# Sixteen instead of twelve places for the norms' small tiles: every later operand lies 128 bytes further on

## The chip, the cores and the metric

The kernel runs on one core of one Trainium2 chip. The metric is the device time of one execution in microseconds, as the median of several runs. TensorE is called PE (its weight loads PEld), VectorE DVE, ScalarE ACT, GpSimd POOL and SyncE SP.

## The reference, cut to what matters

Two layers over 512 tokens of width 1024. Each layer is a half SwiGLU block, a mixer (RWKV-7 with memory attention in the first layer, dilated attention with memory attention in the second), and a second half SwiGLU block:

```python
def swiglu_ffn(x, norm_g, w_in, w_out):
    gate, up = jnp.split(rms_norm(x, norm_g) @ w_in, 2, axis=-1)
    return (jax.nn.silu(gate) * up) @ w_out
...
x = x + 0.5 * swiglu_ffn(x, ...)      # before and after the mixer, in both layers
```

`w_in` is 1024 x 5632 and `w_out` 2816 x 1024. There are four such blocks, and they hold most of the matmuls. In what follows the products with `w_in` are the **first products** and those with `w_out` the **second products**.

## The kernel before

Activations lie transposed: features on the 128 partitions, the 512 tokens along the free axis. A product is made in three passes: every operand is split into a high part, rounded to the matmul's type, and a low rest (`uh`, `ul` for the normed state, `hh`, `hl` for the hidden layer, `kvh`, `kvl` for the state that makes the shared keys and values, `mh`, `ml` for the memory, `whi`, `wlo` for weights), and high x high, high weight x low operand and low weight x high operand add up in one PSUM bank. Each of these is one matmul with 128 columns of weights and, but for the memory, 512 moving columns:

```python
for ps, hi, lo in two:                                      # dense(), lines 424 to 437
    self.nc.tensor.matmul(ps, hi[:, k - c], xh, start=first, stop=False)
    self.nc.tensor.matmul(ps, hi[:, k - c], xl, start=False, stop=False)
    self.nc.tensor.matmul(ps, lo[:, k - c], xh, start=False, stop=last)
```

`weight()` brings the weights in chunks of four 128 x 128 blocks: SP loads `raw` (256 KB, six places), ACT writes `whi`, and DVE or POOL writes `wlo` (four places each). `ffn()` makes 22 pairs of gate and up tiles with eight blocks each (1056 matmuls of first products; the two tiles of a pair take turns by chunk), and then eight output tiles with 22 blocks each (528 matmuls of second products, 66 in a row into one bank; a tile's last chunk has two blocks). With four blocks there are 4224 and 2112 of them. The products of the mixers go through the same `dense()`; in the second mixer, those for the queries take `uh` and `ul`, those for keys and values take `kvh` and `kvl`.

`roots()` makes the per-head norms. Its result is a tile of 4 x 2 numbers per partition, 32 bytes, from a ring in the pool of the state:

```python
ROOTS = 12
r = self.xp.tile([P, 4, 2], F32, tag="roots", bufs=ROOTS, name=self.nm("roots"))[:, :nb]
```

Within a partition the pools lie one behind the other: constants, weights, state, and behind the state the pools that are opened and closed with a block or a mixer. The `roots` ring is the last thing in the state's pool. So its length sets where all later pools begin. Every tile of 512 numbers is 2048 bytes long and every weight block 512 bytes, so that in one pool all of them keep the same start modulo 512 bytes. As the program is laid out, these starts modulo 512 are:

| operand | before | after |
|---|---|---|
| `whi`, `wlo`, `uh`, `ul`, `sq` (weights' and state's pools) | 160 | 160 |
| constants (`cst`) | 288 | 288 |
| `hh`, `hl` (the four blocks) | 32 | 160 |
| `kvh`, `kvl`, `mh`, `ml` | 32 | 160 |
| second mixer: temporaries (`tmp`), `q`, keys, values, `prob` | 32 | 160 |
| first mixer: `tmp`, `krv` | 256 | 384 |
| first mixer: `AR`, `beta`, `kappa`, `mb`, `tx`, `TT` | 320 | 448 |

The order of the work on each engine is written out at build time (`weave()` picks among strands of the mixers by a planner's clock; the blocks are plain loops). The planner does not see the `roots` ring.

Of the kernel before, what the change touches and what calls it, by code (L numbers as in the profile page):

```python
# [223 lines left out]
        return r  # L224


ROOTS = 12
WAIT, FREE = "wait", "free"


# [118 lines left out]
class Net:  # L349
# [206 lines left out]
    def roots(self, sq, n, bank, wide, *change):  # L556
# [3 lines left out]
        for b in range(nb):  # L560
            nc.tensor.matmul(ps[:, b], sq[:, b * P:(b + 1) * P], self.pair, start=True, stop=True,
                             skip_group_check=True)
        r = self.xp.tile([P, 4, 2], F32, tag="roots", bufs=ROOTS, name=self.nm("roots"))[:, :nb]
        nc.vector.tensor_scalar(r, ps, *change[:2], **{f"op{i}": o for i, o in enumerate(change[2:])})
# [778 lines left out]
```

## Time and profile before

| | us |
|---|---|
| median of 3 runs (2123.22 to 2123.34) | 2123.32 |
| the profiled execution, whole | 2117.79 |
| its span, first to last instruction | 2116.0 |

The profile is of one execution. A matmul's record begins when its columns begin to enter and ends when its result is written, so records of matmuls that follow each other overlap: what a matmul costs PE in a row of them is the distance from one start to the next, not the length of its record. In the names of the rows the output stands first, then the moving operand, then the weights: `fps<-hh,whi` is a second product of `hh` with `whi` into a bank `fps`. All instructions carry the line of one helper (L295), so groups are told apart by their tiles' names.

### The profile page before, as it was taken

Reading aid. Unit: us, or ns where it says so; the run is one execution under the profiler, and the core shown is the slowest. Engines: PE = TensorE matmul, PEld = TensorE weight load, DVE = VectorE, ACT = ScalarE, POOL = GpSimd, SP = SyncE. Lnnn points to the kernel's source line nnn. Section 1 sums busy time; section 2 is a strip of 40 time slices with the busy share of each in tenths; the row PEclk is TensorE's granted clock in tenths of the full one; section 3 lists DMA queues with packets and bytes.
Section 4 is the critical chain, followed back from the end, with each engine's and each line's share of the span. In section 5 each row is a group of like instructions: output and inputs, shape, how many; then the busy total and the mean of one; then the engine's idle time right before and its main releaser. Section 6 shows DMA issues by size and latency. Waiting matters only on the chain. (4 is left out here: it accounts for less than half of the span.)

```text
span 2116.0 us, 35895 instructions
## 1 busy us (share of the span) xinstructions
PE 2068.4 (98%) x14582; PEld 1662.6 (79%) x14582; DVE 872.1 (41%) x1300; ACT 813.3 (38%) x1416; POOL 587.7 (28%) x513
## 2 busy tenths in 40 slices
PE   8999999989999999999999999999999999999999
PEld 6888888867677677788888888888787768888887
DVE  6333333454555455333433533333326375333322
ACT  6333333433334544333433433333336554333321
POOL 2222222553332152222222222222232224222221
PEclk9999999999999999999999999999999999999999
DMA  5332344411110173443344433334431154333342
GB/s 195 100 95 95 95 123 131 122 47 35 35 33 26 36 249 114 131 150 98 108 134 126 148 95 100 95 102 124 145 103 51 41 165 159 95 96 99 102 123 80
DMA packets 130645, 222.07 MB, mean 105 GB/s; under 512 B 14232, under 2 KB 31824, under 8 KB 130480
## 3 DMA queue, kind: packets, MB, share of 16 engines
q1 hardware_dynamic: 130480, 219.78, 34.0%
q8 instruction: 114, 1.87, 0.4%
q14 instruction: 51, 0.42, 0.1%
HBM read 202.84 MB, written 21.61 MB: 106 GB/s over the span
## 5 line engine op out<-in xcount | busy, mean ns | idle before, releaser
L295 POOL TENSOR_TENSOR wlo<-raw,whi 128x512 fp32r<-128x512 f32 (+3 forms) x404 | 494.5, 1225 | 1422.7 <-ACT whi L295 1412.2
L295 ACT ACTIVATE whi<-raw 128x512 fp32r<-128x512 f32 (+3 forms) x684 | 416.2, 610 | 938.9 <-PE fps L295 792.3
L295 PE MATMUL fps<-uh,whi 128*128 128x512 f32 x1408 | 551.6, 392 | 7.6 <-ACT whi L295 7.6
L295 PE MATMUL fps<-uh,wlo 128*128 128x512 f32 x1408 | 549.7, 390 | 2.1 <-POOL wlo L295 1.8
L295 PE MATMUL fps<-ul,whi 128*128 128x512 f32 x1408 | 548.9, 390 | 0.0
L295 DVE TENSOR_TENSOR wlo<-raw,whi 128x512 fp32r<-128x512 f32 x280 | 201.8, 721 | 355.4 <-ACT whi L295 346.4
L295 PEld LDWEIGHTS fps<-uh,whi 128*128 128x128 f32 x1408 | 264.8, 188 | 67.7 <-ACT whi L295 11.2
L295 PEld LDWEIGHTS fps<-uh,wlo 128*128 128x128 f32 x1408 | 264.8, 188 | 60.2 <-POOL wlo L295 3.9
L295 PEld LDWEIGHTS fps<-ul,whi 128*128 128x128 f32 x1408 | 264.9, 188 | 55.8 <-issue 0.7
L295 PE MATMUL fps<-hh,wlo 128*128 128x512 f32 x704 | 278.1, 395 | 0.0
L295 PE MATMUL fps<-hh,whi 128*128 128x512 f32 x704 | 278.1, 395 | 0.0
L295 PE MATMUL fps<-hl,whi 128*128 128x512 f32 x704 | 278.1, 395 | 0.0
L295 DVE TENSOR_TENSOR gs<-fps,rstd 128x512 f32<-128x512 f32 x88 | 60.5, 690 | 322.9 <-PE fps L295 322.9
L295 PEld LDWEIGHTS fps<-hh,wlo 128*128 128x128 f32 x704 | 132.2, 188 | 32.2
L295 PEld LDWEIGHTS fps<-hl,whi 128*128 128x128 f32 x704 | 132.2, 188 | 32.1
L295 PEld LDWEIGHTS fps<-hh,whi 128*128 128x128 f32 x704 | 132.2, 188 | 31.9
L295 PE MATMUL mm<-uh,whi 128*128 128x512 f32 x280 | 123.0, 439 | 1.0 <-DVE x L295 0.7
L295 PE MATMUL mm<-ul,whi 128*128 128x512 f32 x280 | 113.2, 404 | 0.0
L295 PE MATMUL mm<-uh,wlo 128*128 128x512 f32 x280 | 112.3, 401 | 0.0
L295 DVE TENSOR_TENSOR hm<-fps,gs 128x512 f32<-128x512 f32 x88 | 60.6, 691 | 121.2 <-PE fps L295 115.4
L295 DVE TENSOR_TENSOR hl<-hm,hh 128x512 fp32r<-128x512 f32 x88 | 77.2, 880 | 51.1 <-ACT hh L295 51.0
L295 PEld LDWEIGHTS mm<-uh,whi 128*128 128x128 f32 x280 | 53.2, 190 | 17.5 <-issue 4.6
(259 smaller groups left out, 2044.0 us busy)
## 6 DMA issues: line engine op xcount, KB each, us to landing
raw<-w SPq DMA_DIRECT2D x512, 256.0 KB, 2.6
raw<-wa_in SPq DMA_DIRECT2D x44, 256.0 KB, 2.7
xd<-x SPq DMA_DIRECT2D x40, 256.0 KB, 2.9
tmp<-xd SPq DMA_DIRECT2D x32, 256.0 KB, 3.2
xin<-xd SPq DMA_DIRECT2D x32, 256.0 KB, 4.3
raw<-w_kv SPq DMA_DIRECT2D x24, 256.0 KB, 2.6
raw<-w SPq DMA_DIRECT2D x32, 128.0 KB, 2.2
raw<-wmem SPq DMA_DIRECT2D x16, 256.0 KB, 2.6
```

The costliest lines, as they stand in the source:

```text
L295: r = f(*args, **kw)
```

## The change

The ring gets 16 places of 32 bytes instead of 12. That is 128 bytes more, and every tile behind it moves by 128 bytes. On each engine, the instructions, their order and the semaphores that they wait on are the same before and after, row for row; addresses alone differ.

```diff
-ROOTS = 12
+ROOTS = 16
```

## Rows read from the trace of the kernel before

**Rows 1.** The page: span, busy time by engine, and granted clock in 40 slices

```profile
span 2116.0 us, 35895 instructions
PE 2068.4 (98%) x14582; PEld 1662.6 (79%) x14582; DVE 872.1 (41%) x1300; ACT 813.3 (38%) x1416; POOL 587.7 (28%) x513
PEclk9999999999999999999999999999999999999999
```

**Rows 2.** Windows of 100 us: span of window, length, PE busy (matmuls), clock, DMA, GB/s

```profile
60.00:160.00 100.00, 100.00 (x442) 1.00 0.31 97
260.00:360.00 100.00, 100.00 (x430) 1.00 0.43 125
1200.00:1300.00 100.00, 100.00 (x443) 1.00 0.33 101
2000.00:2100.00 100.00, 100.00 (x430) 1.00 0.40 119
```

**Rows 3.** Timeline, first products: start us, length us, engine, line, operation; 158 rows between

```profile
20.84 0.39 PE L295 MATMUL fps<-uh,whi 128*128 128x512 f32 x1
...
56.88 0.39 PE L295 MATMUL fps<-uh,whi 128*128 128x512 f32 x1
```

**Rows 4.** The tile `hh`, 252 to 376 us: count, shortest/median/longest ns, first to last start

```profile
L295 PE MATMUL fps<-hh,whi x176: 392/394/398, 252.5 to 375.0; 128*128 128x512 f32 x176
```

**Rows 5.** Timeline, second mixer: queries (10 matmuls between), then keys (7 between)

```profile
1526.70 0.39 PE L295 MATMUL mm<-uh,whi 128*128 128x512 f32 x1
...
1529.19 0.39 PE L295 MATMUL mm<-uh,wlo 128*128 128x512 f32 x1
...
1546.65 0.40 PE L295 MATMUL mm<-kvh,whi 128*128 128x512 f32 x1
...
1548.51 0.39 PE L295 MATMUL mm<-kvh,wlo 128*128 128x512 f32 x1
```

**Rows 6.** Timeline, first mixer's last products; 13 matmuls between the first and the last

```profile
761.21 0.63 PE L295 MATMUL py<-AR,whi 128*128 128x512 f32 x2
...
764.47 0.39 PE L295 MATMUL py<-AR,wlo 128*128 128x512 f32 x1
```

**Rows 7.** Timeline, first products behind another matmul; 11, then 3 matmuls between

```profile
906.45 0.40 PE L295 MATMUL fps<-ul,whi 128*128 128x512 f32 x1
...
909.23 0.39 PE L295 MATMUL fps<-ul,whi 128*128 128x512 f32 x1
...
910.13 0.39 PE L295 MATMUL fps<-uh,wlo 128*128 128x512 f32 x1
```

**Rows 8.** Groups in 253 to 375 us: busy us, mean ns, then idle before and releaser

```profile
L295 PE MATMUL fps<-hl,whi 128*128 128x512 f32 x175 | 69.1, 395 | 0.0
L295 ACT ACTIVATE whi<-raw 128x512 fp32r<-128x512 f32 x40 | 25.2, 631 | 61.4 <-PE fps L295 61.4
L295 POOL TENSOR_TENSOR wlo<-raw,whi 128x512 fp32r<-128x512 f32 x16 | 20.7, 1294 | 65.2 <-ACT whi L295 65.2
```

**Rows 9.** The chain that ended last, its last link (start, length, engine, count)

```profile
1759.71 351.79 PE fps L295 x1533
```

**Rows 10.** Timeline, memory's products of the first layer; 20 matmuls between

```profile
375.70 0.28 PE L295 MATMUL fps<-mh,whi 128*128 128x256 f32 x1
...
378.19 0.28 PE L295 MATMUL fps<-mh,whi 128*128 128x256 f32 x1
```

**Rows 11.** Groups of PE over the whole span, columns as in rows 8

```profile
L295 PE MATMUL sc<-cst,tmp 128*128 128x2 f32 x224 | 28.2, 248 | 0.0
L295 PE MATMUL sc<-TT,tx 32*32 32x32 f32 x1728 | 24.8, 198 | 6.5 <-issue 4.2 <-DVE tx L295 2.2
L295 PE MATMUL sc<-cst,tmp 128*128 128x128 f32 x168 | 23.5, 280 | 1.6 <-ACT tmp L295 1.6
L295 PE MATMUL sc<-tx,mb 32*32 32x32 f32 x1728 | 22.6, 194 | 12.6 <-DVE tx L295 10.5 <-ACT krv L295 1.8
L295 PE MATMUL sc<-cst,prob 128*128 128x128 f32 x96 | 12.7, 276 | 0.1
L295 PE MATMUL sc<-cst,krv 128*128 128x128 f32 x56 | 9.3, 303 | 0.4 <-DVE TT L295 0.4
```

## The prediction, made before the changed kernel ran

> **What bounds the kernel now.** The page first: PE is busy for 98% of the span, no other engine for half of it, and the granted clock is full nearly everywhere [rows 1]. So time can go only where PE's matmuls themselves get quicker. The windows come next. In 100 us of first products PE starts some 442 matmuls, in 100 us of second products 430, PE is busy for 100.00 of 100 us in all four windows, and the granted clock reads 1.00 in each, the 2.4 GHz level [rows 2]. The same matmul (128 columns of weights, 512 moving) thus has two paces, and neither a wait nor the clock makes the difference. The timeline gives them exactly. First products: from 20.84 to 56.88 us are 159 steps, 36.04 / 159 = 226.7 ns. Second products: 176 matmuls of `hh` with `whi`, one in three, start from 252.5 to 375.0 us, which is 175 x 3 = 525 steps, 122.5 / 525 = 233.3 ns [rows 3, 4]. At 2.4 GHz these are 544 and 560 cycles: 16 cycles, or 6.67 ns, per matmul.
>
> **What sets the pace.** First and second products differ in two things: the start of the moving operand modulo 512 bytes (160, as the weights', against 32), and the run of matmuls into one bank (12, then the other tile, against 66). The second mixer separates them, since its queries and its keys go tile by tile through one and the same loop, 24 matmuls into one bank, with moving operands at 160 and at 32. Queries step by (1529.19 - 1526.70) / 11 = 226.4 ns, keys by (1548.51 - 1546.65) / 8 = 232.5 ns [rows 5]. The first mixer's last products, with moving operands at 320 and 256, step by (764.47 - 761.21) / 14 = 232.9 ns [rows 6]. So the quick pace goes with the start, not with the bank. Even at 160 it is not there at once: behind a matmul of another shape the first 12 steps take (909.23 - 906.45) / 12 = 231.7 ns each, and only then (910.13 - 909.23) / 4 = 225 ns, the quick pace to the rows' last digit [rows 7]. It looks like two streams of reads (the moving columns, and the 512 bytes of the next block of weights) that settle into a phase without collisions when they begin alike; this picture is mine, and the sum needs only the paces.
>
> **The change part by part.** It removes and adds no instruction, and order and semaphores stay. It moves addresses.
>
> 1. *Second products.* `hh` and `hl` go from 32 to 160, where `uh`, `ul` and the weights are. They have no idle time ahead of them [rows 8], and behind the last first product nothing of another shape comes between, so the pace should be quick from the start. Four blocks x 528 matmuls x 6.67 ns = **14.1 us**. Ends: nothing if the pace doesn't change (rival A), and 14.1 us, since no row of such a matmul has a quicker steady pace.
> Of this all should reach the end. The last 352 us of the chain are first and second products of the last block alone, 1533 links without a wait [rows 9]. Weights can follow: in the second products ACT waits 61.4 of 122 us for PE to give back a place of `whi`, and POOL 65.2 us for ACT [rows 8], while a chunk would be wanted only 3% sooner; DMA there moves 125 GB/s at 43% of its engines, which would be 129 [rows 2].
>
> 2. *Products of keys and values, and the last products of the second mixer.* Twelve tiles of eight blocks take `kvh` and `kvl`, and eight tiles of four blocks their places afterwards: (96 + 32) x 3 = 384 matmuls, from 32 to 160. These stand among small matmuls, where the quick pace is reached late or not. Lower end 0, upper end 384 x 6.67 = 2.6 us. I take 4 ns each, **1.5 us**, between the two, since runs of 24 are longer than the 12 steps of settling but often broken.
>
> 3. *Memory's products.* 192 matmuls with 256 moving columns, `mh` and `ml` from 32 to 160, now at (378.19 - 375.70) / 21 = 118.6 ns [rows 10]. No row shows such a matmul at the weights' start. Ends 0 and 192 x 6.67 = 1.3 us; I take the middle, **0.6 us**.
>
> 4. *Products with constants.* The constants stay at 288 and the mixers' temporaries move, so here the distance changes and does not become zero: in the first mixer from -32 to +96, in the second from -256 to -128. Nothing says which way the pace goes. The four largest groups are 224 + 168 + 96 + 56 = 544 matmuls [rows 11]; at 6.67 ns each that is 3.6 us more or less. I take 0.
>
> 5. *The ring itself.* Four more places could only take a wait away, and no wait of the program changes. Zero. The loads and stores by DMA and the operands of the other engines move by 128 bytes, too; in the second products these engines wait for PE, not PE for them [rows 8], which covers it. Without that cover a slower `wlo` would show as a wait of PE at a chunk.
>
> Sum: 14.1 + 1.5 + 0.6 = 16.2 us. It is made against the profiled execution (2117.8 us whole, 2116.0 span, and 1.8 us around it), which is 5.5 us under the median of the runs; the matmuls' count is the same in every execution, so I take the same 16.2 us off the median: 2123.3 - 16.2 = **2107.1 us**, 0.76% less.
>
> One rule speaks against the change. The Trainium skill says in "TensorE: Matmul & The Clock Gate" (Step-by-step: what each phase is for) that PE reads moving columns and weights through two independent ports, so that loading the next weights takes nothing from the running matmul, and in "SBUF — State Buffer" (Who interferes with whom) that "PE and ACT never wait on anyone". By that a start address is worth nothing and the time stays at 2123.3 us, which is rival A's; the first page's distance of N / 2.4 + 2.5 ns would be 215.7 ns for 512 columns. This trace disagrees: it has 226.7 and 233.3 ns where that rule knows one figure, and the two paces of rows 5 within one loop.
>
> **The rivals.**
>
> A. *No change.* The slow pace belongs to something else in the second products, the 66 matmuls in a row into one bank, or to where `hh` lies at large (some 70 KB and more behind the weights in a partition, while `uh` follows them directly). Then the keys need another cause, and terms 2 and 3 fall too: 2123.3, with term 4 between 2119.7 and 2126.9. For it: the second products have no faithful twin in the trace, and queries and keys lie in different places as well. Against it: the three unlike groups off the start 160 (32, 256, 320) all step by 232.5 to 233.3 ns.
>
> B. *The pace settles only half the time.* A tile of second products ends with a chunk of two blocks, and if that breaks the phase as another shape does [rows 7], 12 of 66 steps stay slow: 14.1 x 12 / 66 = 2.6 us of the gain go, 2109.7, still within the range. If it breaks at every chunk, of 11 steps on average where rows 7 show 12 to settle, I halve term 1: 2123.3 - 7 = 2116. Against it: the first products change tile and bank every 12 matmuls and keep 226.7 ns.
>
> C. *Slower.* The pace belongs to where an operand lies by itself, not to the distance from the weights, and the moved operands of the mixers land badly: term 4 at its bad end, 3.6 us, and the 3456 matmuls of 32 x 32 in the solver [rows 11], whose operands go from 320 to 448, four at a time, 3456 / 4 x 6.67 = 5.8 us. Together 9.4 us. Beside a whole term 1 that still leaves 2116.5; it decides from the point where term 1 is under 9.4 us, and with none of it the time is 2132.7. For it: no row shows a start of 384 or 448. Against it: in those groups both operands move together, and 160 is quick in every row.
>
> **How the numbers follow.** Forecast 0.85; A 0.08; B at 2116 0.04; C at 2132.7 0.03. The range: at best terms 1 to 3 at their upper ends and term 4 in our favour, 14.1 + 2.6 + 1.3 + 3.6 = 21.6 us, 2101.7; at worst of the forecast term 1 alone with term 4 against us, 14.1 - 3.6 = 10.5 us, 2112.8. I take 2101 to 2113, which also holds B's milder form; A, C and B's strong form, 0.15, are left out. A measurement of this kernel can tell about 0.2%, 4.2 us: faster means below 2119.1, which the forecast and B are, 0.89; A is within, 0.08; C is slower, 0.03.
>
> **What would show it.** In the profile after, `hh`'s 176 matmuls with `whi` in a block should start over 525 x 0.2267 = 119.0 us instead of 122.5, and 100 us of second products should hold some 442 matmuls. The first products should keep 226.7 ns. The keys should come near the queries' pace. The last products of the first mixer (to 448 and 384) should stay near 233 ns; if they too go to 226.7, the equal start is not the cause. I am wrong if the second products keep 233.3 ns, or if they reach 226.7 and the mixers give it back: then the stretches between the blocks would have grown.

## The result and the profile after

The changed kernel takes 2108.93 us (median of six runs, 2105.84 to 2109.45), the kernel before, beside it, 2123.33 us. The ratio is 0.9928, with a 95% interval from 0.9916 to 0.9941: 14.4 us faster, between 12.5 and 17.8. The forecast was 16.2 us: 2107.1 us, in a range from 2101 to 2113.

The page of the kernel after (compare [rows 1]): span and instructions, busy time by engine, granted clock in 40 slices.

```profile
span 2107.2 us, 35895 instructions
PE 2058.1 (98%) x14582; PEld 1665.5 (79%) x14582; DVE 872.1 (41%) x1300; ACT 813.1 (39%) x1416; POOL 588.6 (28%) x513
PEclk9999999989999999999999999999999999999999
```

PE is busy for the same 98% (idle for 47.6 us of the span before and 49.1 us after): the matmuls themselves have become shorter. Of a matmul's record only the start is used here, since the profiler models its end. The windows of the kernel after show it (columns: window, length, PE busy with its matmuls, granted clock, DMA share, GB/s). Two hold first products (60 and 1200 us), two second products (260 and 2000 us).

```profile
60.00:160.00 100.00, 100.00 (x443) 1.00 0.32 97
260.00:360.00 100.00, 100.00 (x442) 1.00 0.44 128
1200.00:1300.00 100.00, 100.00 (x443) 1.00 0.30 95
2000.00:2100.00 100.00, 100.00 (x443) 1.00 0.39 113
```

The second products now start as many matmuls in 100 us as the first, where [rows 2] had 430 against 442, at the same full clock. The group of `hh` with `whi` in the first block of the kernel after (shortest, median and longest record in ns, first and last start) answers to [rows 4]:

```profile
L295 PE MATMUL fps<-hh,whi x176: 389/389/389, 253.0 to 372.0; 128*128 128x512 f32 x176
```

That is 119.0 / 525 = 226.7 ns from start to start, from the first step of the block to the last. The chain that ended last still closes with one run of PE (start, length, matmuls of its last link): 360.12 / 1584 = 227.3 ns each, where [rows 9] gave 351.79 / 1533 = 229.5.

```profile
1742.62 360.12 PE fps L295 x1584
```

**The profiled executions differ by less.** Their whole times are 2117.79 us before and 2109.01 after, 8.8 us apart, not 14.4. The four blocks alone gave 14.0 us there, so something else took time in the execution after. The same kernel ran again in a later job (sixteen places again, below), and its profile has a span of 2103.0 us, 4.2 less than the one after, with the same instructions at the same addresses. These rows show where (first-mixer matmuls of `uh` with `wlo`, first and last start in the profiles of before, after, and sixteen places again):

```profile
L295 PE MATMUL mm<-uh,wlo x216: 387/393/796, 388.9 to 761.0; 128*128 128x512 f32 x108
```

```profile
L295 PE MATMUL mm<-uh,wlo x216: 387/395/796, 386.0 to 761.5; 128*128 128x512 f32 x108
```

```profile
L295 PE MATMUL mm<-uh,wlo x216: 387/393/792, 385.9 to 759.5; 128*128 128x512 f32 x108
```

The stretch takes 372.1, 375.5 and 373.6 us. It is one in which the granted clock falls to its lower level, 1.2 GHz, for some time, while PE works on mostly small matmuls with waits between them. Its window in the profiles of before and after (window, length, busy time and count of PE, PEld, DVE, ACT and POOL, granted clock, DMA share, GB/s):

```profile
388.00:761.00 373.00, 346.18 (x6707) 263.69 (x6706) 192.60 (x346) 150.05 (x293) 141.58 (x149) 0.98 0.17 53
```

```profile
388.00:761.00 373.00, 345.92 (x6690) 262.12 (x6689) 191.01 (x344) 147.07 (x287) 139.33 (x141) 0.97 0.16 51
```

How long the clock is low differs between executions: the traces' records of the clock hold 23 us at the lower level in the whole span before, 36 us after and 24 us in the repetition. The eleven profiles kept of kernels (before, after and experiments, with 12, 16 and 24 places) in which `uh`, `ul` and the weights begin alike show what that does to the stretch: with 14 us of it at the lower level it takes 371.2 and 371.3 us, with 17 us 372.1 and 372.7, with 21 us 372.7 to 373.7, with 24 us 374.7 and 375.5, with 27 us 376.8. So the stretch grows with the time at the lower level, whichever ring the kernel has, and one kernel gets more of it in one execution than in another. The 8.8 us hold some microseconds of a clock that the change did not set, and the median of the runs is what counts.

### The profile page after: what moved, and what is told of

Its sections match the earlier page's. It is cut to its first block, busy times and chain, and to the rows that moved or that the text cites. A ratio compares the mean times of both kernels' runs of the same rounds, so it can differ in the third digit from the quotient of the medians.

```text
span 2107.2 us, 35895 instructions
## 1 busy us (share of the span) xinstructions
PE 2058.1 (98%) x14582; PEld 1665.5 (79%) x14582; DVE 872.1 (41%) x1300; ACT 813.1 (39%) x1416; POOL 588.6 (28%) x513
```

## The experiments

The median of the kernel before was 2122.36 us in the job of the first four experiments (20 runs, 2116.14 to 2126.5) and 2120.16 us in the job of the last four (7 runs); the single run beside the four in between took 2126.62 us. "Distance" is in what follows the start of a moving operand minus the start of the weights, in bytes. All four blocks get their hidden layer from a pool of their own, so a tile put at the head of that pool moves `hh` and `hl`, the other tiles of that pool (`gs`, `hm` and, in the first two blocks, `mh` and `ml`), and nothing else:

```diff
+            if FFN_PAD.get(which):
+                hp.tile([P, FFN_PAD[which] // 4], F32, tag="pad", bufs=1, name=self.nm("pad"))
```

**Only the hidden layer moves.** Ring of 12 places, and 128 bytes ahead of `hh` in each block.

```diff
+FFN_PAD = {'00': 128, '01': 128, '10': 128, '11': 128}
```

> Ring of 12 places as before; an unused tile of 128 bytes at the head of the four blocks' pool moves hh and hl (and mh, ml) from 32 to 160, all else stays. Theory (the second products' pace is the whole gain, as term 1 says): second products at 226.7 ns, 119.0 us instead of 122.5 in a block, 2123.3 - 14.1 = 2109.2 us, keys still near 232 ns. Rival (the longer ring or the shifted mixers bring part of the 14.4 us measured): less than 14.1 comes, above 2111 us.

Measured: 2106.38 us, ratio 0.9930 (0.9904 to 0.9957), the same as with the whole change. Windows of first and of second products:

```profile
60.00:160.00 100.00, 100.00 (x443) 1.00 0.32 98
265.00:365.00 100.00, 100.00 (x443) 1.00 0.45 131
```

The keys keep their slow step (232.2 ns on average, as before). The gain is the second products'; the other terms are too small to be seen in a time.

**Everything moves but the hidden layer.** Ring of 16 places, and 384 bytes ahead of `hh`, which puts it back at 32 modulo 512.

```diff
-ROOTS = 12
+ROOTS = 16
+FFN_PAD = {'00': 384, '01': 384, '10': 384, '11': 384}
```

> Ring of 16 places, everything moved as in the changed kernel, but a tile of 384 bytes at the head of the blocks' pool puts hh and hl (and mh, ml) back to 32 modulo 512. Theory: second products back at 233.3 ns; of the gain only the keys' and values' share is left, 2123.3 - 1.5 = 2121.8 us. Rival (ring or mixers): several us of the gain stay, 2119 us or less.

Measured: 2122.67 us, ratio 0.9999 (0.9988 to 1.0009).

```profile
60.00:160.00 100.00, 100.00 (x443) 1.00 0.32 98
265.00:365.00 100.00, 100.00 (x430) 1.00 0.43 126
```

Of the whole change, without the hidden layer's place, nothing is left that the runs can tell. The keys do step by 228.7 ns here, but their 1 to 2 us are less than the runs can tell.

**Distance or place?** Two kernels with a ring of 12 places tell them apart. In the first, the state's pool alone begins 128 bytes later: `uh` and `ul` are 128 bytes off the weights, and everything behind, `hh` too, is moved to 160. In the second, the weights' pool begins 128 bytes later as well, so that weights, `uh` and `ul` all start at 288, and `hh` at 160.

```diff
+        self.xp.tile([P, 32], F32, tag="xpad", bufs=1, name="xpad")
```

> Ring of 12; an unused tile of 128 bytes at the head of the state's pool: weights at 160, uh and ul at 288, hh and hl at 160, keys' operands at 160. Theory (the distance from the weights counts): first products 4224 x 6.67 = 28.2 us slower at 233.3 ns, second products 14.1 us quicker at 226.7 ns, the mixers' products of uh 840 x 4 ns = 3 us slower: about 2123.3 + 28.2 - 14.1 - 1.5 + 3 = 2139 us. Rival (the gain is peculiar to the second products, or to operands that lie far from the weights): first products stay at 226.7 ns, 2108 us.

```diff
+        self.wp.tile([P, 32], F32, tag="wpad", bufs=1, name="wpad")
```

> Ring of 12; an unused tile of 128 bytes at the head of the weights' pool: weights, uh and ul at 288, hh and hl at 160, keys' operands at 160; the only difference from the run with uh alone off is where the weights lie. Theory (distance from the weights): first products 226.7 ns, second products 233.3 ns, as before the change, 2123 us. Rival (a moving operand at 160 is quick by itself, wherever the weights are): first products 233.3, second products 226.7 ns, 2139 us as with uh alone off.

Measured: 2132.24 us, ratio 1.0041 (1.0024 to 1.0059), and 2120.31 us, ratio 0.9994 (0.9981 to 1.0006). The windows of the first kernel:

```profile
60.00:160.00 100.00, 100.00 (x432) 1.00 0.30 95
265.00:365.00 100.00, 100.00 (x443) 1.00 0.44 126
```

And of the second:

```profile
60.00:160.00 100.00, 100.00 (x442) 1.00 0.32 98
265.00:365.00 100.00, 100.00 (x431) 1.00 0.44 127
```

In the first the two kinds of products have changed roles: first products slow, second quick. In the second the first products are quick again, although `uh` lies at 288 as in the first, and the second products are slow with `hh` at 160, the place that is quick in the changed kernel. So the distance counts and not an operand's own place. The first kernel lost less than forecast, since its first products step by 232.4 ns, not 233.3 (why, no run tells): 4224 x 5.7 ns = 24.1 us, less the 14.0 us that the second products gain, is 10.1 us. The mixers' products of `uh` and `ul` lose some 2 us more (840 x 2.6 ns) and the keys gain 1.3 us, which makes 11 us; 2132.24 - 2122.36 = 9.9 us were measured, between 5 and 12.5.

**The pace at all distances.** Three kernels with a ring of 12 places, each with four distances, one in each block, and one run each.

```diff
+FFN_PAD = {'00': 32, '01': 64, '10': 96, '11': 160}
```

> Ring of 12; unused tiles of 32, 64, 96 and 160 bytes at the head of the pool of the first, second, third and fourth block put hh and hl at 64, 96, 128 and 192: 96, 64, 32 bytes ahead of and 32 behind the weights' start modulo 512. Theory (pace is quick where moving operand and weights begin alike modulo 512): no block at 226.7 ns, all between 232 and 233.3 ns (122.2 to 123.0 us from first to last start). Rival (the distance costs gradually): the nearest distances, 32 bytes, lie clearly nearer to 226.7 ns than the 128 bytes of before, at about 228.3 ns if in proportion.

```diff
+FFN_PAD = {'00': 192, '01': 256, '10': 320, '11': 384}
```

> As the scan before, hh and hl at 224, 288, 352 and 416: 64, 128, 192 and 256 bytes behind the weights' start modulo 512. Theory: none at 226.7 ns, all 232 to 233.3 ns. Rival (what counts is the distance modulo 256): the fourth block, at 256, at 226.7 ns, 119.5 us from first to last start instead of 123.

```diff
+FFN_PAD = {'00': 416, '01': 448, '10': 480, '11': 352}
```

> As the scan before, hh and hl at 448, 480, 0 and 384: 224, 192 and 160 bytes ahead of and 224 behind the weights' start modulo 512. Theory: none at 226.7 ns, all 232 to 233.3 ns. Rival (there are better distances than 0): one of them under 226.7 ns.

Times: 2118.77, 2113.18 and 2118.91 us. The pace of a block is again its group's last start minus its first, over 525 steps. Blocks at the distances -96, -64, -32 and +32, first kernel:

```profile
L296 PE MATMUL fps<-hh,whi x176: 392/397/400, 253.0 to 376.0; 128*128 128x512 f32 x176
L296 PE MATMUL fps<-hh,whi x176: 394/394/394, 1038.4 to 1160.9; 128*128 128x512 f32 x176
L296 PE MATMUL fps<-hh,whi x176: 395/396/397, 1402.6 to 1525.1; 128*128 128x512 f32 x176
L296 PE MATMUL fps<-hh,whi x176: 393/396/399, 1989.1 to 2111.6; 128*128 128x512 f32 x176
```

+64, +128, +192 and +256, second kernel:

```profile
L296 PE MATMUL fps<-hh,whi x176: 394/394/398, 253.0 to 373.2; 128*128 128x512 f32 x176
L296 PE MATMUL fps<-hh,whi x176: 392/394/398, 1038.5 to 1161.0; 128*128 128x512 f32 x176
L296 PE MATMUL fps<-hh,whi x176: 394/394/394, 1401.9 to 1524.4; 128*128 128x512 f32 x176
L296 PE MATMUL fps<-hh,whi x176: 389/389/389, 1987.1 to 2106.1; 128*128 128x512 f32 x176
```

-224, -192, -160 and +224, third kernel:

```profile
L296 PE MATMUL fps<-hh,whi x176: 393/396/399, 253.4 to 375.9; 128*128 128x512 f32 x176
L296 PE MATMUL fps<-hh,whi x176: 394/394/397, 1042.4 to 1162.6; 128*128 128x512 f32 x176
L296 PE MATMUL fps<-hh,whi x176: 392/392/398, 1404.1 to 1526.6; 128*128 128x512 f32 x176
L296 PE MATMUL fps<-hh,whi x176: 395/396/397, 1989.3 to 2111.8; 128*128 128x512 f32 x176
```

Put together, with the distance taken modulo 256:

| distance modulo 256 | distances that were run | ns per matmul |
|---|---|---|
| 0 | 0, +256 | 226.7 |
| 64 | +64, -192 | 229.0 |
| 160 | -96 | 234.3 |
| 32, 96, 128, 192, 224 | +32, -224; -160; -128, +128; -64, +192; -32, +224 | 233.3 |

Distances that are equal modulo 256 have the same pace, also where they differ modulo 512, and where several distances share one pace, each such pair still has a pattern of steps of its own: at -32 and +224 steps of 231 or 232 ns take turns with 235, at +32 and -224 one step in four is 230 or 231 and the others 233 to 235, and at -64 and +192 all are 233 or 234. So the modulo 512 of the table of starts and of the prediction is twice the true period. No other distance in steps of 32 bytes reaches the pace of 0; finer steps were not tried.

**A ring of 24 places**, so that `hh` lies 256 bytes from the weights' start in the whole kernel, beside sixteen places again.

```diff
-ROOTS = 12
+ROOTS = 24
```

> Ring of 24 places: everything behind the state's pool moves by 384 bytes, hh, hl, keys' operands and mh, ml to 416, which is 256 bytes off the weights' 160. Theory (the distance counts modulo 256, as the single block of the second scan had it): second products 226.7 ns, keys as with 16 places, the same time as the changed kernel, about 2109 us. Rival (modulo 512, as the change's words have it): second products near 233 ns, 2123 us.

```diff
-ROOTS = 12
+ROOTS = 16
```

> The changed kernel once more, beside the ring of 24 places on one chip. Both theories: 2109 us; the first has both within 0.2% of each other, the rival has this one 14 us quicker.

Measured: 2106.59 us, ratio 0.9931 (0.9917 to 0.9946), and 2106.34 us, ratio 0.9935 (0.9917 to 0.9953). The first block's group with 24 places:

```profile
L295 PE MATMUL fps<-hh,whi x176: 389/389/390, 253.9 to 372.9; 128*128 128x512 f32 x176
```

119.0 us as with sixteen. In the whole kernel, too, only the distance modulo 256 counts.

**Which weights collide?** While a matmul streams its columns, PE loads the next block of weights: in the traces the load for a matmul starts some 3 ns behind the start of the matmul before it and lasts 188 ns. With `wlo` 128 bytes off and `whi`, `hh` and `hl` at 160 (`uh` and `ul` come to 288), the three matmuls of a product differ: high x high has `whi` in use and loads `whi`; high weight x low operand has `whi` in use and loads `wlo`; low weight x high operand has `wlo` in use and loads `whi`. One run.

```diff
+        if not self.split:
+            self.wp.tile([P, 32], F32, tag="wpad", bufs=1, name="wpad")
```

> Ring of 12; an unused tile of 128 bytes between whi and wlo: whi at 160, wlo at 288, uh and ul at 288, hh and hl at 160. Of the second products' three steps (whi with hh, whi with hl, wlo with hh) one is out of line. Theory (the moving columns collide with the load of the NEXT block of weights): the step of whi with hl, during which wlo at 288 is loaded, is long, and the two others are 226.7 ns, so that the mean is 228.9 ns. Rival (with the block in use): the step of wlo with hh is long. If the phase between the two streams is lost by one unlike block in three, all three steps are mixed and the mean is 232 to 233.3 ns.

Measured: 2145.05 us; the first products are slow everywhere (233.3 ns). The timeline of second products (start and length in us):

```profile
299.98 0.39 PE L295 MATMUL fps<-hh,whi 128*128 128x512 f32 x1
300.20 0.40 PE L295 MATMUL fps<-hl,whi 128*128 128x512 f32 x1
300.44 0.40 PE L295 MATMUL fps<-hh,wlo 128*128 128x512 f32 x1
300.67 0.39 PE L295 MATMUL fps<-hh,whi 128*128 128x512 f32 x1
```

With the trace's nanoseconds, the steps repeat as 227, 232 or 233, 234 through the whole block, 231.1 ns on average, which no theory had forecast. So high x high is quick, the matmul that loads the off `wlo` is slow, and the one that has it in use is slow too. Neither the block being loaded alone nor the block in use alone explains this.

**Every other chunk off.** Ring of 16 places, and the four places of `whi` and `wlo` each 128 bytes longer, so that the weights of every other chunk are 128 bytes off modulo 256 (`raw` gives one of its six places for it). One run.

```diff
-        hi = self.take(self.wp, [P, WB, P], F32R, "whi", 4)[:, :nb]
-        lo = self.take(self.wp, [P, WB, P], F32R, "wlo", 4)[:, :nb]
+        hi = self.take(self.wp, [P, WB * P + 32], F32R, "whi", 4)[:, :nb * P].rearrange("p (b u) -> p b u", u=P)
+        lo = self.take(self.wp, [P, WB * P + 32], F32R, "wlo", 4)[:, :nb * P].rearrange("p (b u) -> p b u", u=P)
```

> Ring of 16; the four places of whi and of wlo are 128 bytes longer each and raw has five places instead of six, so that the weights of every other chunk lie at 32 and those between at 160 modulo 256, and all moving operands of dense products at 160. Theory N (the moving columns collide with the load of the next block): the long steps begin with the last step of the chunk ahead, during which the first block at 32 is loaded, and end one step before the off chunk ends. Theory U (block in use): they begin and end with the off chunk. Theory P (the two streams hold a phase and lose it): after the off chunk several steps stay long. Mean by N and U (226.7 + 233.3) / 2 = 230 ns, by P more.

Measured: 2135.82 us; first products step by 231.4 ns, second by 230.9 ns on average. The steps in the fourth tile of the first block's second products, in ns, from the trace (chunks of 12 matmuls):

```
chunk 1, aligned: 231 226 227 227 226 227 227 226 227 227 226 233
chunk 2, off:     241 231 232 232 228 230 232 241 233 231 231 233
chunk 3, aligned: 236 224 231 236 228 232 232 226 227 227 226 233
```

The last step of an aligned chunk is long: while it streams, PE loads the first block of the off chunk. So it begins with the block being loaded. It does not end with it: behind an off chunk the aligned one needs seven steps to come back to 227 ns, though nothing that it uses or loads there is off. Behind an off chunk of two blocks, as at the end of the tile before, it needs one: the 231 that opens chunk 1.

**A single operand off.** Ring of 16 places; one of a block's 22 `hh` tiles in a place of its own, 128 bytes off in three blocks and 192 in the second. One run.

```diff
+                if m == 10:
+                    hp.tile([P, 32], F32, tag="pad", bufs=1, name=self.nm("pad"))
+                    hh = hp.tile([P, T], F32R, tag="hx", bufs=1, name=self.nm("hx"))
+                    hp.tile([P, 96], F32, tag="pad2", bufs=1, name=self.nm("pad2"))
```

> Ring of 16; of the 22 tiles hh of a block one, the eleventh, lies 128 bytes (in one block 192) off the weights' start, all hl and the other hh at distance 0. Theory N or U: in each run of 66 only the steps whose moving operand is that tile, the 31st and the 33rd, are long, by some 7 ns: mean 226.9 ns. Theory P: the steps behind them are long, too, up to the 12 steps that the rows of before show behind a matmul of another shape: mean some 228 ns.

Measured: 2104.56 us, with a mean granted clock of 0.995. The timeline around the two matmuls of the first tile that read the off operand (`hx`):

```profile
259.73 0.39 PE L295 MATMUL fps<-hh,wlo 128*128 128x512 f32 x1
259.96 0.40 PE L295 MATMUL fps<-hx,whi 128*128 128x512 f32 x1
260.19 0.39 PE L295 MATMUL fps<-hl,whi 128*128 128x512 f32 x1
260.42 0.40 PE L295 MATMUL fps<-hx,wlo 128*128 128x512 f32 x1
260.65 0.39 PE L295 MATMUL fps<-hh,whi 128*128 128x512 f32 x1
```

The steps from there on, in ns, first block (128 off) and second block (192 off):

```
first block:  234 226 234 226 227 226 227 227 226 227 227 226 227 227 226
second block: 234 226 231 229 229 233 236 224 231 236 228 233 230 226 227
```

At 128 only the two matmuls themselves are long, and the pace is back at once. At 192 the disturbance lasts for 13 steps. So here the distance decides whether anything is left to settle; but it is not the distance alone, since whole chunks at 128 did leave something in the run before.

## Why the prediction was right, point by point

*Term 1, second products, 14.1 us.* Right in mechanism and size: (122.5 - 119.0) x 4 blocks = 14.0 us, at the quick pace from the first step. The first kernel of the experiments has the whole gain with the hidden layer's pool alone, the second has none of it without that. The weights followed, as argued from [rows 8]: ACT's time for `whi` stays hidden, with 59.2 of 119 us in which it waits for PE (group of the kernel after, 253 to 372 us: busy us and mean ns, then idle us ahead and what ended it).

```profile
L295 ACT ACTIVATE whi<-raw 128x512 fp32r<-128x512 f32 x40 | 25.2, 629 | 59.2 <-PE fps L295 59.2
```

*Term 2, keys and values, 1.5 us.* About right. The keys of the kernel after (compare [rows 5]):

```profile
1540.65 0.39 PE L295 MATMUL mm<-kvh,whi 128*128 128x512 f32 x1
...
1542.46 0.39 PE L295 MATMUL mm<-kvh,wlo 128*128 128x512 f32 x1
```

Eight steps in 1.81 us are 226.3 ns, the queries' pace. On average over the undisturbed steps between matmuls of `kvh` and `kvl` (those under 260 ns, 321 of them) it is 228.8 ns, 232.2 before: 3.4 ns, not 4, and 1.3 us.

*Term 3, memory, 0.6 us.* The step that failed, in sign; its lower end, zero, was too high, if by little. The kernel after, compare [rows 10]:

```profile
372.71 0.28 PE L295 MATMUL fps<-mh,whi 128*128 128x256 f32 x1
...
375.22 0.28 PE L295 MATMUL fps<-mh,whi 128*128 128x256 f32 x1
```

2.51 / 21 = 119.5 ns against 118.6. Over all 96 matmuls of each layer the steps went from 118.7 to 119.9 ns in the first and stayed at 119.9 in the second: a loss of 0.1 us. Equal starts don't help a matmul with 256 moving columns here, they are at the slow end: in the scans, where `mh` and `ml` move along with `hh`, the same products step by 117.8 ns at the distances +64, -64, -192 and -224. I had carried the 6.67 ns over from another shape without a row for it.

*Term 4, products with constants, 0 of 3.6 us either way.* Right: their mean steps changed by about 1 ns or less in the large groups (those of `prob`, 113.7 before and 113.5 after); only one small group, `mpr`, got slower by more, 113.0 to 116.6 ns over 25 steps, 0.1 us. One premise was wrong, though: by the period of 256 the change took an equal start from the second mixer's products with constants (256 bytes apart before, 128 after), and of them only `mpr` shows a loss.

*Term 5, the ring, 0.* Right: no engine shows a new wait, and with 24 places the time is that of 16.

*What should stay.* First products: 443 in 100 us, unchanged. The last products of the first mixer, which came to 448 and 384 and stayed unequal to the weights (compare [rows 6]):

```profile
761.78 0.63 PE L295 MATMUL py<-AR,whi 128*128 128x512 f32 x2
...
765.04 0.39 PE L295 MATMUL py<-AR,wlo 128*128 128x512 f32 x1
```

3.26 / 14 = 232.9 ns, to the digit what it was. This kept the equal start as the cause before any experiment.

*The sum.* By the rows it is 14.0 + 1.3 - 0.1 = 15.2 us, against 16.2 forecast and 14.4 (12.5 to 17.8) measured. The time alone could not have told that terms 2 and 3 were too large, by 0.9 us together; the rows do. Nor did it matter that the prediction went by modulo 512: every operand of its terms 1 to 3 came from 128 bytes off to an equal start by either period. *The rivals.* A (no change) fell with the windows after and with the only-the-hidden-layer kernel. B (settles half the time) fell: chunks and tiles of one shape don't disturb the pace, nor does the two-block chunk at a tile's end. C (an operand's own place) fell with the two kernels of distance or place. The rule of two independent ports in the Trainium skill ("TensorE: Matmul & The Clock Gate", Step-by-step: what each phase is for), by which nothing should have happened, is not what these runs show: 226.7 to 234.3 ns for one and the same matmul, by addresses alone. Whether the ports or something behind them is shared, no run tells.

*The sentence on growing mixers.* The prediction would have been wrong if the mixers gave the gain back. In the profile after the first mixer's stretch did grow, by 3.4 us; in the profile of the same kernel in the later job by 1.5 us, while the whole span was 13.0 us shorter than before. It goes with the time at the lower clock, as shown above, and the runs' median keeps the gain.

*What stays open.* How the collision arises. The block being loaded while the columns stream starts it (every other chunk off), but the kernel with `wlo` off has a slow matmul that loads an aligned block, and what a disturbance leaves behind it differs: nothing after one operand 128 off, one or seven steps after a chunk of weights 128 off, some ten after an operand 192 off. My picture of two streams that find a phase fits all of these and is shown by none. None of the other kernels is faster than the changed one by more than runs of one kernel differ (2106.38 and 2106.59 us, and 2104.56 us in a single run, against 2106.34 us of the changed kernel in its second job).

## What to carry to other kernels

Where matmuls of this shape (128 x 128 weights, 512 moving columns of four bytes) follow each other without a gap, let the moving operand and the weight blocks start at the same address modulo 256 bytes in their partitions; a tile of padding at the head of a pool does it, and cost nothing here but its bytes. Look for such a loss in distances from start to start, by groups with like shapes and unlike addresses, since a busy share of 100% and a full clock say nothing of it. A pace found for one shape is not to be carried to another without a row that has it.

## What the runs showed of the hardware

- The pace of a row of matmuls with 128 x 128 weights and 512 moving columns, at the clock's upper level, depends on the distance between moving operand and weights modulo 256 bytes: in the second products 226.7 ns at 0, 229.0 at 64, 234.3 at 160, 233.3 at the other multiples of 32. First products at 128 step by 232.4 ns. At 2.4 GHz that is 544 cycles at best, 560 mostly; why 544 and not 512, no run tells.
- Equal means hide unlike rhythms: in the kernel before, the steps of the second products alternate between 229 and 237 or 238 ns, and at a distance of 192 they are all 233 or 234.
- Among matmuls with equal starts, one with its moving operand 128 bytes off costs 7 ns and nothing behind it; two that are 192 off, two steps apart, disturb the 13 steps from the first of them on.
- With 256 moving columns equal starts gave nothing: 119.9 ns, against 118.7 and 119.9 at 128 bytes off, and 117.8 at +64, -64, -192 and -224.
- The first mixer's stretch, where the granted clock is part of the time at its lower level, took from 371.2 us with 14 us at that level to 376.8 us with 27 us.
